# Seven-product down projection: units worked singly, finer operand splits, two of the six summed weight pieces kept in scratch slots

## The chip, the cores and the metric

The kernel runs on one core of one Trainium2 chip, as one launch. The metric is device time in microseconds (us), from the first to the last work of an execution. Five engines matter: TensorE (PE; its weight loads are listed apart as PEld), VectorE (DVE), ScalarE (ACT), GpSimd (POOL) and SyncE (SP), the last here only to issue plain transfers. Accumulating transfers are issued from GpSimd. All transfers run on the core's sixteen DMA engines.

## The reference

One decoder layer on 512 tokens of width 1024, in float32: RMS norm, one input projection, two mixers (a Mamba-2 SSD group and a forgetting-attention group), an output projection, a residual, and a gated MLP. The change is in the last part:

```python
def conv_gated_mlp(x, w_up, conv_w, conv_b, w_down):
    h = x @ w_up.astype(x.dtype)
    h = causal_depthwise_conv(h, conv_w, conv_b)
    gate, val = jnp.split(h, 2, axis=-1)
    return (jax.nn.silu(gate) * val) @ w_down.astype(x.dtype)

hf = rms_norm(x, norm_ffn_w[layer])
x = x + conv_gated_mlp(hf, w_up[layer], ffn_conv_w[layer], ffn_conv_b[layer], w_down[layer]).astype(x.dtype)
```

Here `w_up` is 1024 x 5632 and `w_down` is 2816 x 1024; the product with `w_down` is 512 x 2816 by 2816 x 1024.

## The kernel before

**Float32 from three passes.** Every large product splits both operands into a high part (a cast to float32r, on ScalarE) and a low part (the value less its high part, a subtraction on VectorE or GpSimd). `mm3` (L108) then does three matmuls: high by high (L110), high by low (L111), low by high (L112).

**The up projection** (`up_proj`, `gated`, `sums`, L734 to L787). 44 weight tiles of 512 KB go through `load_split` (L99): a load into one of five `wraw` slots, the cast and the subtraction. For each of the eleven values of j (L789) two tiles of the first half of the MLP's width and then two of the second half are projected, scaled by the token norm `R2`, convolved (L768 to L773) and gated (L775, and the product on GpSimd in L780 and L791). The result g is the left operand; its quarters over (first or second half of the tokens) x (first or second half of the 2816) are formed at once: `a11` and `a12` as high and low parts, `a22` and the four sums `S1` to `S4` as plain float32 (L792 to L794, L780 to L787). The squares for the token norm go into a scratch tile `junk` (L751), of the pool `pu`, which lives only as long as the up projection.

**The down projection** (L798 to L876) multiplies 2 x 2 blocks in seven products instead of eight. A weight quarter (B11, B12, B21, B22) is 1408 x 512: eleven k tiles, laid out as six units, five of two k tiles (512 KB) and one of a single k tile. `PRODUCTS` (L815) lists for each product its weight (a quarter, or None for the sum held in T), the next left operand, its two PSUM tiles, whether it starts or continues them, and where the result is added to `x2` (L874). Products 0, 1 and 6 read B11, B21 and B22 through `wraw` slots (`load_unit`, L713). Products 2 to 5 read T, six SBUF pieces that hold a running sum of quarters: `fresh` (L805) loads a quarter piece into T from SP, `gather` (L808) adds another one to it by an accumulating transfer from GpSimd. `next_sum` (L825) says which: B11 + B12 for product 2, then + B22 for product 3, + B21 for product 4, then B22 + B12 anew for product 5. (Signs lie in the left operands and in the additions.) A piece can be overwritten only when its split for the running product is done.

For each unit the loop of L844 calls `split_unit` (L720: cast on ScalarE, subtraction on VectorE, into one of three slots for `wh` and `wl`), then `next_sum`, then, at units 1 to 3, a third of the split of the next product's left operand (`split_into`, L755), and then the unit's matmuls, 12 for a unit of two k tiles. Units 4 and 5 are held and their 18 matmuls done together, ordered by output tile, at every product's end (L853 to L858). T is a pool of its own (L802), opened when `pu` has been closed.

**What sets the order.** The engines run their instructions in order. A planner lays out each engine's order before the run, from program order and from a timeline of its own; so a piece of work may stand earlier or later on its engine than its place in the program. SP and GpSimd have one queue each: what stands behind a waiting instruction waits too.

Of the kernel before, what the change touches and what calls it, by code (L numbers as in the profile page):

```python
# [8 lines left out]
F32 = mybir.dt.float32  # L9
F32R = mybir.dt.float32r  # L10
AF = mybir.ActivationFunctionType
ALU = mybir.AluOpType
# [3 lines left out]
P = 128  # L16
SEQ = 512
D = 1024
# [37 lines left out]
def tile_hybrid_layer(  # L56
# [19 lines left out]
    nc = tc.nc  # L76
# [11 lines left out]
    def raw(ap):  # L88
        return ap.bitcast(F32)
# [18 lines left out]
    def mm3(o, ah, al, bh, bl, start, stop, grouped=True):  # L108
        kw = {} if grouped else {"skip_group_check": True}
        pe.matmul(o, ah, bh, start=start, stop=False, **kw)  # L110
        pe.matmul(o, ah, bl, start=False, stop=False, **kw)  # L111
        pe.matmul(o, al, bh, start=False, stop=stop, **kw)  # L112

    def bank(name="g"):
        return pg.tile([P, 512], F32, tag="g", name=name)
# [572 lines left out]
    pb = ctx.enter_context(tc.tile_pool(name="pb", bufs=1, reuse_waits="tile"))  # L688
    NH = NFF // 2
# [3 lines left out]
    def operand(slot=None):  # L693
        if slot is None:
            hl_ = [pb.tile([P, NH, HT], F32R, tag=t, name=t, bufs=2) for t in ("oh", "ol")]
            return hl_[0], hl_[1]
        pair_ = [pxt.tile([P, NK, SEQ], F32R, tag=t, name="o" + t) for t in ("xh", "xl")]
        return tuple(
            t.rearrange("p a b -> p (a b)")[:, 0 : NH * HT].rearrange("p (a b) -> p a b", b=HT) for t in pair_
        )  # L700
# [6 lines left out]
    UNITS = [(k, min(k + 2, NH)) for k in range(0, NH, 2)]  # L707
    B11, B12, B21, B22 = 0, 1, 2, 3

    def part(q, u):  # L710
        return wdown[q, :, UNITS[u][0] * 512 : UNITS[u][1] * 512]

    def load_unit(q, u):  # L713
        rw = wp.tile([P, 1024], F32, tag="wraw", name="wraw", bufs=5)
        nc.sync.dma_start(rw[:, 0 : (UNITS[u][1] - UNITS[u][0]) * 512], part(q, u))
        return rw

    turn = [0]

    def split_unit(u, src):  # L720
        n = (UNITS[u][1] - UNITS[u][0]) * 512
        where = pb if turn[0] % 3 == 2 else wp
        turn[0] += 1
        h = where.tile([P, 1024], F32R, tag="wh", name="wh")
        l = where.tile([P, 1024], F32R, tag="wl", name="wl")
        act.copy(h[:, :n], src[:, :n])  # L726
        dve.tensor_tensor(out=l[:, :n], in0=src[:, :n], in1=raw(h[:, :n]), op=ALU.subtract)  # L727
        return h, l

    pu_ctx = ExitStack()  # L730
    pu = pu_ctx.enter_context(tc.tile_pool(name="pu", bufs=1, reuse_waits="tile"))
# [16 lines left out]

    early = up_proj((0, NFF), 2)
    for tb in range(NTB):  # L750
        junk = pu.tile([P, D], F32, tag="junk", name="junk", bufs=2)  # L751
        act.activation(junk, x2[:, tb, :], AF.Square, accum_out=ss[:, tb : tb + 1])
    token_scale(r2, R2, ss, pu)

    def split_into(o, src, lo, hi):  # L755
        act.copy(o[0][:, lo:hi, :], src[:, lo:hi, :])
        dve.tensor_sub(o[1][:, lo:hi, :], src[:, lo:hi, :], raw(o[0][:, lo:hi, :]))

    def gated(j):
        both = []  # L760
        for part in range(2):
            f = part * NFF + j
            o = early[part] if j == 0 else up_proj((f,), 1)[0]
            xp = pu.tile([P, SEQ], F32, tag="up", name="up", bufs=3)
            dve.tensor_mul(xp, o, R2)  # L765
            a = pu.tile([P, SEQ], F32, tag="ua", name="ua", bufs=5)
            cw = C_FCW + 3 * f
            act.activation(a, xp, AF.Identity, scale=pc[:, cw + 2 : cw + 3], bias=pc[:, C_FCB + f : C_FCB + f + 1])  # L768
            for s in range(1, 3):
                dve.scalar_tensor_tensor(  # L770
                    out=a[:, s:], in0=xp[:, : SEQ - s], scalar=pc[:, cw + 2 - s : cw + 3 - s], in1=a[:, s:],
                    op0=ALU.mult, op1=ALU.add,
                )  # L773
            both.append(a)
        act.activation(both[0], both[0], AF.Silu)  # L775
        return both

    def sums(j, g, k, val):
        g1, g2 = g[:, 0:HT], g[:, HT:]
        pool.tensor_tensor(out=k, in0=k, in1=val, op=ALU.mult)  # L780
        k1, k2 = k[:, 0:HT], k[:, HT:]
        act.copy(a12[0][:, j, :], k1)
        dve.tensor_sub(a12[1][:, j, :], k1, raw(a12[0][:, j, :]))
        act.copy(a22[:, j, :], k2)
        pool.tensor_tensor(out=S1[:, j, :], in0=g2, in1=k2, op=ALU.subtract)
        pool.tensor_tensor(out=S2[:, j, :], in0=S1[:, j, :], in1=g1, op=ALU.subtract)
        pool.tensor_tensor(out=S4[:, j, :], in0=k1, in1=S2[:, j, :], op=ALU.add)  # L787

    for j in range(NH):  # L789
        g, val = gated(j)  # L790
        pool.tensor_tensor(out=g, in0=g, in1=val, op=ALU.mult)  # L791
        act.copy(a11[0][:, j, :], g[:, 0:HT])  # L792
        dve.tensor_sub(a11[1][:, j, :], g[:, 0:HT], raw(a11[0][:, j, :]))
        pool.tensor_tensor(out=S3[:, j, :], in0=g[:, 0:HT], in1=g[:, HT:], op=ALU.subtract)  # L794
        k, val = gated(j + NH)
        if j < NH - 1:
            sums(j, g, k, val)
    ready = [split_unit(u, load_unit(B11, u)) for u in range(3)]  # L798
    sums(NH - 1, g, k, val)
    pu_ctx.close()  # L800

    pt_ = ctx.enter_context(tc.tile_pool(name="pt", bufs=1, reuse_waits="tile"))  # L802
    T = [pt_.tile([P, 512 * (b - a)], F32, tag="T%d" % a, name="T%d" % a) for a, b in UNITS]

    def fresh(q, u):  # L805
        nc.sync.dma_start(T[u], part(q, u))

    def gather(q, u):  # L808
        nc.gpsimd.dma_start(T[u], part(q, u), accum_op=ALU.add)

    Y, Z, X1, X2 = (
        [mbank("Y") for _ in range(2)], [mbank("Z") for _ in range(2)], [bank("X") for _ in range(2)], None
# [9 lines left out]
        (B22, S4, Z, False, ((0, 512, ADD, True),)),  # L822
    )

    def next_sum(n, u):  # L825
        if n == 0:
            fresh(B11, u)
            gather(B12, u)
        elif n in (2, 3):
            gather(B22 if n == 2 else B21, u)  # L830
        elif n == 4:
            fresh(B22, u)
            gather(B12, u)

    ops = [a11, a12]
    for n, (quarter, _, tiles, start, adds) in enumerate(PRODUCTS):
        nxt = PRODUCTS[n + 1][1] if n + 1 < len(PRODUCTS) else None
        if nxt is not None:
            ops.append(operand(1 if n % 3 == 1 else None))
        tiles = [bank("X") for _ in range(2)] if tiles is None else tiles  # L840
        lhs = ops[n]
        final = n == len(PRODUCTS) - 1
        held = []
        for u, (lo, hi) in enumerate(UNITS):  # L844
            if n == 0 and u < len(ready):
                h, l = ready[u]
            else:
                h, l = split_unit(u, T[u] if quarter is None else load_unit(quarter, u))
            next_sum(n, u)
            if nxt is not None and u in (1, 2, 3):  # L850
                split_into(ops[n + 1], nxt, 4 * (u - 1), min(4 * u, NH))
            held.append((lo, hi, h, l))
            if u == len(UNITS) - 2:  # L853
                continue
            todo = [(k, i, b) for b in held for k in range(b[0], b[1]) for i in range(2)]
            held = []
            if u == len(UNITS) - 1:
                todo.sort(key=lambda t: t[1])  # L858
            for k, i, (lo_, _, h_, l_) in todo:
                c = slice((k - lo_) * 512, (k - lo_ + 1) * 512)  # L860
                s = slice(i * P, (i + 1) * P)
                mm3(
                    tiles[i], lhs[0][:, k, s], lhs[1][:, k, s], h_[:, c], l_[:, c], start and k == 0, k == NH - 1,
                    grouped=False,
                )
                if k == NH - 1:
                    for row, col, op, done in adds:
                        tb = row + i
                        cuts = 2 if final and i == 1 else 1
                        w = 512 // cuts  # L870
                        for cut in range(cuts):
                            c = slice(cut * w, (cut + 1) * w)
                            oc = slice(col + cut * w, col + (cut + 1) * w)
                            dve.tensor_tensor(out=x2[:, tb, oc], in0=x2[:, tb, oc], in1=tiles[i][:, c], op=op)  # L874
                            if done:
                                nc.sync.dma_start(out[tb * P : (tb + 1) * P, oc], x2[:, tb, oc])  # L876
# [14 lines left out]
def _lay_out(i, np):  # L891
# [3 lines left out]
    def cols(v):  # L895
        return v.reshape(-1, 128).T

    def taps(v):
# [20 lines left out]
        "x": x,  # L919
        "xT": x.T.reshape(8, 128, 512),  # L920
        "wdtf": dtf.reshape(8, 128, 32).transpose(1, 0, 2).reshape(128, 256),
# [32 lines left out]
```

## Time and profile before

| | |
|---|---|
| median of 3 runs | 847.28 us (845.74 to 851.2) |
| the profiled execution | 845.59 us, span 843.8 us |
| granted TensorE clock | 0.998 |
| TensorE busy | 810.0 us (96%) |
| VectorE, ScalarE, GpSimd busy | 75%, 52%, 35% |
| up projection on TensorE | about 482 to 722.7 us |
| the seven products on TensorE | 722.7 to 839 us |
| accumulating transfers (T, from GpSimd) | 24: 20 of 512 KB, 4 of 256 KB |
| plain loads of T (from SP) | 12: 10 of 512 KB, 2 of 256 KB |

Times in the rows are microseconds from the span's start; the second number of a timeline row is the duration, and the bracket at its end gives the idle time before it and what ended that. In a row of a group stand busy time and mean nanoseconds of one. Matmuls are pipelined, so a busy TensorE isn't one at its peak: the steps from one matmul's start to the next tell more. In a table by windows the number in brackets is the count of instructions, and the DMA share is the mean busy share of the sixteen DMA engines, where overlapping packets can make it a little over 1.

### The profile page before, as it was taken

The numbers are of one execution on the slowest core, as the hardware profiler recorded it, in microseconds if no ns is written. First come the engines' busy times: TensorE is split into PE (matmuls) and PEld (weight loads), VectorE is DVE, ScalarE is ACT, GpSimd is POOL, SyncE is SP. The second block draws the span as 40 slices with busy tenths as digits, with TensorE's granted clock in tenths as the row PEclk, the third lists the DMA queues.
The fourth block names the chain that finished last, engine by engine and source line by source line (L and its number), as shares of the span: only waits on it lengthen the run. The fifth ranks groups of instructions, "written<-read, shape, count | busy, mean of one in ns | idle before, by whom it ended". The sixth has DMA issues, their size and how long they took to land.

```text
span 843.8 us, 12403 instructions
## 1 busy us (share of the span) xinstructions
PE 810.0 (96%) x4590; PEld 696.6 (83%) x4590; DVE 630.9 (75%) x999; ACT 434.6 (52%) x830; POOL 291.4 (35%) x281
## 2 busy tenths in 40 slices
PE   6999989899989999999999999999999999998987
PEld 4888879779989898798898888888888888875766
DVE  7696998775779788997988767666666667875644
ACT  5456546443567675684575364444444444654432
POOL 3125253375445445135133413333333331332210
PEclk9999999999999999999999999999999999999999
DMA  8424322431442332333331222322222333599972
GB/s 313 164 76 130 100 101 76 133 105 50 140 123 86 104 101 92 96 112 107 95 101 51 95 81 100 99 99 89 91 97 100 100 100 109 160 304 240 241 169 88
DMA packets 32285, 101.63 MB, mean 120 GB/s; under 512 B 4129, under 2 KB 4961, under 8 KB 32225
## 3 DMA queue, kind: packets, MB, share of 16 engines
q1 hardware_dynamic: 28768, 89.31, 32.3%
q0 software_dynamic: 3456, 11.54, 7.0%
q8 instruction: 36, 0.59, 0.3%
q14 instruction: 25, 0.20, 0.1%
HBM read 94.44 MB, written 2.20 MB: 115 GB/s over the span
## 4 chain that ended last, share of the span: by engine, by line
PE 67%; DVE 13%; issue 7%; DMA 6%; POOL 3%; ACT 3%; SPq 0%; DVEq 0%; POOLq 0%; ACTq 0%
PE up L112 9%; PE up L110 9%; PE up L111 9%; DMA T<-in_wdown_dram 4%; PE pq L111 4%; PE pq L112 4%; PE pq L110 4%; PE po L112 3%; PE po L111 3%; PE po L110 3%; DVE xs L351 2%; PE o L580 1%; PE pT L566 1%; POOL ms L122 1%; PE Y L111 1%
## 5 line engine op out<-in xcount | busy, mean ns | idle before, releaser
L104 ACT CAST wh<-wraw 128x1024 fp32r<-128x1024 f32 x103 | 108.4, 1053 | 135.5 <-PE up L111 72.1
L110 PE MATMUL pq<-wh,xh 128*128 128x256 f32 x512 | 146.3, 288 | 0.0
L112 PE MATMUL pq<-wh,xl 128*128 128x256 f32 x512 | 146.2, 286 | 0.0
L111 PE MATMUL pq<-wl,xh 128*128 128x256 f32 x512 | 145.3, 284 | 0.6 <-DVE wl L105 0.6
L112 PE MATMUL up<-hh,wl 128*128 128x512 f32 (+1 forms) x368 | 140.2, 381 | 0.2 <-DVE wl L105 0.2
L111 PE MATMUL up<-hl,wh 128*128 128x512 f32 (+1 forms) x368 | 139.9, 380 | 0.0
L110 PE MATMUL up<-hh,wh 128*128 128x512 f32 (+1 forms) x368 | 139.8, 380 | 0.0
L105 POOL TENSOR_TENSOR wl<-wraw,wh 128x1024 fp32r<-128x1024 f32 x31 | 75.3, 2427 | 107.7 <-ACT wh L104 98.6
L105 DVE TENSOR_TENSOR wl<-wraw,wh 128x1024 fp32r<-128x1024 f32 x72 | 90.3, 1254 | 20.0 <-ACT wh L104 19.9
L111 PEld LDWEIGHTS pq<-wl,xh 128*128 128x128 f32 x512 | 97.8, 191 | 2.1 <-DVE wl L105 1.1
L110 PEld LDWEIGHTS pq<-wh,xh 128*128 128x128 f32 x512 | 97.5, 191 | 1.9 <-issue 1.2
L112 PEld LDWEIGHTS pq<-wh,xl 128*128 128x128 f32 x512 | 97.8, 191 | 0.7 <-issue 0.5
L112 PEld LDWEIGHTS up<-hh,wl 128*128 128x128 f32 x368 | 69.2, 188 | 13.8 <-DVE wl L105 0.4
L111 PEld LDWEIGHTS up<-hl,wh 128*128 128x128 f32 x368 | 69.2, 188 | 13.1
L110 PEld LDWEIGHTS up<-hh,wh 128*128 128x128 f32 x368 | 69.1, 188 | 13.1 <-issue 0.2
L765 DVE TENSOR_TENSOR up<-up,R 128x512 f32<-128x512 f32 x44 | 30.3, 691 | 57.0 <-PE up L112 57.0
L770 DVE SCALAR_TENSOR_TENSOR ua<-up,pc,ua 128x511 f32<-128x511 f32 (+1 forms) x88 | 67.1, 765 | 3.2 <-ACT ua L768 1.7
L526 POOL TENSOR_SCALAR bias<-cum,tokS 128x256 f32<-128x256 f32 (+1 forms) x32 | 22.4, 711 | 88.9 <-DVE nm L541 88.9
L254 DVE TENSOR_TENSOR x<-po,x 128x512 f32<-128x512 f32 x64 | 43.2, 683 | 10.1 <-PE po L112 9.5
L545 ACT ACTIVATE prob<-prob,nm 128x128 f32<-128x128 f32 (+1 forms) x64 | 35.9, 562 | 27.2 <-DVE nm L541 26.9
L780 POOL TENSOR_TENSOR ua<-ua 128x512 f32<-128x512 f32 x11 | 15.0, 1364 | 93.0 <-DVE ua L770 93.0
L727 DVE TENSOR_TENSOR wl<-T,wh 128x1024 fp32r<-128x1024 f32 (+1 forms) x24 | 26.9, 1134 | 26.2 <-ACT wh L726 26.2
(249 smaller groups left out, 1876.9 us busy)
## 6 DMA issues: line engine op xcount, KB each, us to landing
wraw<-in_wup_dram SPq DMA_DIRECT2D x44, 512.0 KB, 3.3
wraw<-in_wqkv_dram SPq DMA_DIRECT2D x24, 512.0 KB, 3.3
T<-in_wdown_dram POOLq DMA_DIRECT2D x20, 512.0 KB, 11.9
wraw<-in_wout_dram SPq DMA_DIRECT2D x16, 512.0 KB, 3.4
wraw<-in_wdown_dram SPq DMA_DIRECT2D x15, 512.0 KB, 4.6
wraw<-in_wxbc_dram SPq DMA_DIRECT2D x11, 512.0 KB, 4.0
T<-in_wdown_dram SPq DMA_DIRECT2D x10, 512.0 KB, 8.0
wraw<-in_wz_dram SPq DMA_DIRECT2D x8, 512.0 KB, 3.4
```

Of the source, the lines that this page charges most:

```text
L104: act.copy(h, r)
L105: (sub or dve).tensor_tensor(out=l, in0=r, in1=raw(h), op=ALU.subtract)
L110: pe.matmul(o, ah, bh, start=start, stop=False, **kw)
L111: pe.matmul(o, ah, bl, start=False, stop=False, **kw)
L112: pe.matmul(o, al, bh, start=False, stop=stop, **kw)
L254: dve.tensor_add(dst, o, dst)
L351: dve.scalar_tensor_tensor(out=dst[:, s:], in0=xp[:, : SEQ - s], scalar=half_w[:, cw + 3 - s : cw + 4 - s], in1=dst[:, s:], op0=ALU.mult, ...
L526: (dve if qb == 2 else pool).tensor_scalar(out=b, in0=cum[:, :n], scalar1=-1.0, scalar2=edge, op0=ALU.mult, op1=ALU.add)
L545: act.activation(p, p, AF.Exp, scale=-1.0, bias=nm[:, qb : qb + 1], accum_out=sm[:, qb : qb + 1])
L727: dve.tensor_tensor(out=l[:, :n], in0=src[:, :n], in1=raw(h[:, :n]), op=ALU.subtract)
L765: dve.tensor_mul(xp, o, R2)
L770: dve.scalar_tensor_tensor(out=a[:, s:], in0=xp[:, : SEQ - s], scalar=pc[:, cw + 2 - s : cw + 3 - s], in1=a[:, s:], op0=ALU.mult, op1=ALU.add,
```

## The change

Three things in the down projection; the products, their order and their sums are the same.

1. Every unit's matmuls follow its own split. Units 4 and 5 are held together only in the last product.
2. The next left operand is split at every unit, by the unit's own k tiles: five pieces of 512 columns and one of 256, instead of pieces of 1024, 1024 and 768 columns at units 1 to 3.
3. `junk` moves from the pool `pu` to the lasting pool `pb`. After its last use its two slots hold T[0] and T[1], whose load and gather for product 2 (B11, then B12) are written into the program after the first three loads of B11 and before the last `sums`; T[2] to T[5] stay in the later pool.

```diff
+    T = []
+    def fresh(q, u):
+        nc.sync.dma_start(T[u], part(q, u))
+    def gather(q, u):
+        nc.gpsimd.dma_start(T[u], part(q, u), accum_op=ALU.add)
...
-        junk = pu.tile([P, D], F32, tag="junk", name="junk", bufs=2)
+        junk = pb.tile([P, D], F32, tag="junk", name="junk", bufs=2)
...
+        if j == NH - 2:
+            T = [pb.tile([P, 1024], F32, tag="junk", name="T", bufs=2) for _ in range(2)]
     ready = [split_unit(u, load_unit(B11, u)) for u in range(3)]
+    for u in range(2):
+        fresh(B11, u)
+        gather(B12, u)
     sums(NH - 1, g, k, val)
     pu_ctx.close()
...
-    T = [pt_.tile([P, 512 * (b - a)], F32, tag="T%d" % a, name="T%d" % a) for a, b in UNITS]
+    T += [pt_.tile([P, 512 * (b - a)], F32, tag="T%d" % a, name="T%d" % a) for a, b in UNITS[2:]]
...
+    ADDED = {0: B12, 2: B22, 3: B21, 4: B12}
     def next_sum(n, u):
+        if n == 0 and u < 2:
+            return
+        if n in (0, 4):
+            fresh(B11 if n == 0 else B22, u)
+        if n in ADDED:
+            gather(ADDED[n], u)
...
-            if nxt is not None and u in (1, 2, 3):
-                split_into(ops[n + 1], nxt, 4 * (u - 1), min(4 * u, NH))
+            if nxt is not None:
+                split_into(ops[n + 1], nxt, lo, hi)
             held.append((lo, hi, h, l))
-            if u == len(UNITS) - 2:
+            if final and u == len(UNITS) - 2:
                 continue
...
-            if u == len(UNITS) - 1:
+            if final and u == len(UNITS) - 1:
                 todo.sort(key=lambda t: t[1])
```

More of the change, by code (lines that the diff above doesn't have):

```diff
@@ L802, in tile_hybrid_layer @@
     pt_ = ctx.enter_context(tc.tile_pool(name="pt", bufs=1, reuse_waits="tile"))
-    T = [pt_.tile([P, 512 * (b - a)], F32, tag="T%d" % a, name="T%d" % a) for a, b in UNITS]
[L805 to L809, printed above, removed]
+    T += [pt_.tile([P, 512 * (b - a)], F32, tag="T%d" % a, name="T%d" % a) for a, b in UNITS[2:]]
     Y, Z, X1, X2 = (
@@ L823, in tile_hybrid_layer @@
     )
+    ADDED = {0: B12, 2: B22, 3: B21, 4: B12}
     def next_sum(n, u):
[L826 to L833, printed above, removed]
+        if n == 0 and u < 2:
[4 more added lines that the diff above has]
+            gather(ADDED[n], u)
     ops = [a11, a12]
```

## The prediction

> **What bounds the kernel now.** I read the page first, then the chain of waits, then the last 120 us in 8 us windows, then each engine's and each DMA queue's order in time there.
>
> ```profile
> span 843.8 us, 12403 instructions
> core 0: 843.8 us, clock 0.998
> ```
>
> The profiled execution took 845.59 us, 1.8 us more than its span; the median of the three timed runs is 847.28. The granted clock is full, so nothing here is a matter of the clock. The chain shows the matmul rhythm and the limits of the down stage:
>
> ```profile
> 540.44 0.23 PE up L110
> 554.72 0.23 PE up L110
> 722.68 0.45 PE Y L110 x2
> 838.72 0.24 PE Z L112
> 755.89 17.31 DMA T<-in_wdown_dram
> 800.65 11.36 DMA T<-in_wdown_dram
> ```
>
> The first two rows are 63 matmuls apart (L110 is every third): 14.28 / 63 = 0.2267 us each. The seven products hold 7 x 11 x 2 x 3 = 462 matmuls, 104.7 us; they take from 722.68 to 838.96, 116.3 us. So TensorE loses 11.5 us in this stage, and that is all an edit of the operand traffic can win. Where it loses them:
>
> ```profile
> core 0: us, PE busy (x) PEld busy (x) DVE busy (x) ACT busy (x) POOL busy (x), PEclk, DMA share, GB/s
> 724.00:732.00 8.00, 8.00 (x37) 6.57 (x36) 7.10 (x8) 4.92 (x7) 2.25 (x2) 1.00 0.49 135
> 740.00:748.00 8.00, 7.62 (x34) 5.95 (x33) 6.32 (x6) 3.29 (x4) 4.93 (x6) 1.00 1.05 328
> 756.00:764.00 8.00, 7.62 (x33) 5.77 (x32) 5.04 (x5) 2.54 (x3) 2.47 (x3) 1.00 1.06 276
> 764.00:772.00 8.00, 6.79 (x26) 4.27 (x24) 2.76 (x3) 2.72 (x3) 1.70 (x2) 1.00 1.08 252
> 772.00:780.00 8.00, 6.13 (x25) 4.34 (x25) 7.20 (x9) 5.68 (x6) 1.70 (x2) 1.00 1.06 211
> 788.00:796.00 8.00, 7.62 (x33) 5.93 (x33) 7.07 (x8) 5.58 (x6) 0.00 (x0) 1.00 1.05 257
> 804.00:812.00 8.00, 5.64 (x22) 3.52 (x21) 3.65 (x4) 2.09 (x2) 1.73 (x2) 1.00 1.07 244
> ```
>
> An unhindered window starts 37 matmuls. Against that, 764 to 780 lacks 23 (5.2 us), 804 to 812 lacks 15 (3.4 us), and 740, 756 and 788 lack 3, 4 and 4 (2.5 us together). The DMA share is at 1.05 to 1.08 in all of them, against 0.49 before: the sixteen DMA engines are full. So the two large losses are waits for T, and the whole stretch is a DMA backlog that TensorE drains.
>
> **The change, part by part.** *The DMA ledger.* The price of one 512 KB unit, from stretches where one queue has the engines nearly alone (775 to 787 for the accumulating queue, which has them quite alone; 735 to 745 for loads):
>
> ```profile
> q0 software_dynamic: 762, 2.52, 107.1%
> q1 hardware_dynamic: 994, 3.27, 91.3%
> q0 software_dynamic: 33, 0.14, 7.2%
> ```
>
> A gather: 2.52 MB in 12 us is 0.210 MB/us, so 0.524 MB take 2.50 us. A plain load: 3.27 MB in 10 x 91.3 / 98.5 = 9.27 us, so 1.49 us. [...]
>
> The backlog starts when the first T pieces are loaded and ends when the last gathered piece is cast:
>
> ```profile
> 732.79 4.36 SPq L806 DMA_DIRECT2D T<-in_wdown_dram  x6
> 818.36 0.62 ACT L726 CAST wh<-T 128x512 fp32r<-128x512 f32 x1 [0.19 <-DMA T<-in_wdown_dram]
> ```
>
> In those 85.6 us the queues carry two plain quarters into T (11 units), half of B21's last unit pair and five units of B22 fetched ahead (5.5), one unit of output, and four gathered quarters (22): 17.5 x 1.49 + 22 x 2.50 = 81.1 us. The other 4.5 us are loads already in flight at 732.8 and completion. It is a saturated queue from end to end.
>
> *What is moved.* T[0] and T[1] get the scratch slots of `junk`, and their load and gather (B11 + B12, units 0 and 1) stand in the program before the last `sums`. The slots are long free, and SP has room:
>
> ```profile
> L752 ACT ACTIVATE junk<-x x4: 1045/1050/1065, 485.4 to 488.6; 128x1024 f32<-128x1024 f32 x4
> 703.07 6.77 SPq L715 DMA_DIRECT2D wraw<-in_wdown_dram  x2
> L806 SPq DMA_DIRECT2D T<-in_wdown_dram x12: 327/379/946, 732.8 to 800.1; - x12
> DMA to landing us min/median/max: 4.4/8.5/11.6
> 716.92 1.30 POOL L791 TENSOR_TENSOR ua<-ua 128x512 f32<-128x512 f32 x1 [8.52 <-DVE ua L770]
> ```
>
> The third of the three loads that precede them goes out at 703.07; two more issues of 0.38 us follow, land between 708 and 715.5 (4.4 to 11.6 us later), and their gathers run under the up projection, where the DMA share is about half (the 0.49 above). That takes 2 x (1.49 + 2.50) = 8.0 us out of the ledger. The new wait is GpSimd's: a gather waits for its load, and the gate products (L791, L780) and the last sums are queued behind it. Landed by 715.5, they come before L791's start at 716.92. If SP lets one more load ahead (the second of the two in that row, at 709.5) and the maximum of 11.6 us applies, L791 starts some 4 us late, at 721; its result is the eleventh k of product 0, wanted at 722.68 + 60 x 0.2267 = 736.3. I cost it at nothing under that cover of 15 us; without it the 4 us would stand in product 0.
>
> *Units worked singly.* Now units 4 and 5 (18 matmuls) are held together at every product's end and both their operand slots come free at the end; then unit 4's slot comes free 6 matmuls, 1.36 us, earlier. *Smaller splits.* The split of the next left operand goes from pieces of 1024, 1024 and 768 columns at units 1 to 3 to five of 512 and one of 256 at units 0 to 5. The wall it makes today:
>
> ```profile
> 739.68 3.22 DVE L757 TENSOR_TENSOR ol<-sum,oh 128x1024 fp32r<-128x1024 f32 x3
> 742.82 3.49 DVE L727 TENSOR_TENSOR wl<-wraw,wh 128x1024 fp32r<-128x1024 f32 x3
> 744.10 0.50 PE L111 MATMUL X<-wl,oh 128*128 128x512 f32 x1 [0.39 <-DVE wl L727]
> L757 DVE TENSOR_TENSOR ol<-sum,oh 128x1024 fp32r<-128x1024 f32 x4 | 4.7, 1218 | 0.0
> 733.88 0.96 DVE L757 TENSOR_TENSOR oxl<-sum,oxh 128x768 fp32r<-128x768 f32 x1 [0.62 <-ACT oxh L756]
> L727 DVE TENSOR_TENSOR wl<-T,wh 128x512 fp32r<-128x512 f32 x4 | 2.8, 688 | 1.3 <-ACT wh L726 1.3
> 697.52 0.42 DVE L793 TENSOR_TENSOR ol<-ua,oh 128x256 fp32r<-128x256 f32 x1
> ```
>
> Three pieces in a row stand ahead of the next wl, and TensorE waits: that is the loss in 740, 756 and 788. VectorE's cost rises from 2 x 1.22 + 0.96 = 3.40 to 5 x 0.69 + 0.42 = 3.87 us a product, 2.3 us over five products; it is 3 to 7 of 8 us busy in the windows above, so this lies in its idle time, and where that cover is gone it is at most 0.47 us a product. The additions into x2 start now 3 instead of 9 matmuls before a product's end; today they stand in VectorE's order behind the whole product anyway, so nothing is charged. Breaking the wall is worth 0 to 2.5 us by itself, less than nothing only in the slow rival.
>
> *The sum.* TensorE's side offers up to 11.5 us, the backlog's side 8.0: the stage ends with the later, so the gain is 8.0. The losses at the walls then hide in the wait for the DMA, as long as it stays full. It should: a gather issued at 755.89 lands 17.3 us later today, nearly all of it queueing; 8 us less leaves 9 us of queue. What is late next is again product 5: unhindered it would begin at 722.68 + 5 x 14.96 = 797.5 (66 matmuls a product), and its last T piece arrives at 818.4 - 8.0 = 810.4, against a need near 797.5 + 60 x 0.2267 - 1.3 = 809.8; so a small wait stays there. Profiled time 845.59 - 8.0 = 837.6; on the median, 847.28 - 8.0 = **839.3**.
>
> **The rivals.**
>
> *TensorE becomes the bound.* Loads of B22 into T go out today at
>
> ```profile
> 787.60 0.34 SPq L806 DMA_DIRECT2D T<-in_wdown_dram  x1
> 800.13 0.33 SPq L806 DMA_DIRECT2D T<-in_wdown_dram  x1
> 796.77 0.86 POOL L809 DMA_DIRECT2D T<-in_wdown_dram  x1 [11.35 <-DMA T<-in_wdown_dram]
> 805.31 1.04 ACT L726 CAST wh<-T 128x1024 fp32r<-128x1024 f32 x1 [5.94 <-DMA T<-in_wdown_dram]
> ```
>
> with a spread of 12.5 us, because the pieces of product 4 came late. Without walls and late sums they go out sooner against the product, the gathers of product 5 meet fewer of them, and all waits vanish: 847.28 - 11.5 = 835.8.
>
> *The load-and-gather chain of product 5 is latency, not queue.* From the load at 787.60 to the cast at 805.31 are 17.7 us, and the load cannot go before product 4 has split T[0]. If those 17.7 us stay, so do product 5's 3.4 us, and with the walls half kept (1.3 us) the gain is 11.5 - 4.7 = 6.8; with the walls whole and a wait of 1 us at each of the units 1 to 3 it is 3: 840.5 to 844.3. [...]
>
> *The early sums are not early.* The planner may place the two loads as late as it does today, behind the loads of B21:
>
> ```profile
> 732.40 0.33 SPq L715 DMA_DIRECT2D wraw<-in_wdown_dram  x1
> ```
>
> Then only the walls can give: 0 to 2.5 us, 845 to 847.
>
> *Slower.* The six small pieces stand one behind each unit's cast on in-order queues. A slot has two units, 5.44 us, from free to needed; a cast and a subtraction with a piece ahead of each need 1.05 + 0.62 + 1.23 + 0.69 = 3.6. If the planner puts two more pieces ahead and the slot's release adds 0.5, TensorE waits on most of the 30 units of products 1 to 5. At 0.27 us each that eats the 8.0; from 0.55 us it is slower by 8.5, and at 0.6 the time is 847.28 - 8.0 + 18 = 857. Against it: the wall of 3.22 us costs TensorE about 0.7 us today, not more.
>
> **How the numbers follow.** The forecast 0.50, with gains from 6 to 10; TensorE as the bound 0.18; latency 0.18; not early 0.08; slower 0.06. One per cent, about what a measurement of this kernel can tell from no change, is 8.5 us, just above the forecast: four tenths of the forecast's own chance lie beyond it. So faster by over 1% is 0.18 + 0.20 and a little for the runs' spread, 0.40; within 1% 0.54; slower 0.06. The range runs from the TensorE bound, 835.8, to the bad end of the latency case, 844.5.
>
> **What would show it.** Product 2's last T piece is cast now at
>
> ```profile
> 766.65 0.62 ACT L726 CAST wh<-T 128x512 fp32r<-128x512 f32 x1 [1.37 <-DMA T<-in_wdown_dram]
> ```
>
> Right: two loads and two gathers of T before 722; that cast near the time it is needed, 752.6 + 12.3 = 764.9, without waiting for a DMA, and no TensorE wait in products 2 and 3; the last T cast near 810; DMA share still above 1 from 740 to 805; no row of three splits in VectorE's order. It is wrong if T still ends near 818 with the first two sums early, if the DMA share falls below 1 in products 3 and 4 (then the stage is TensorE's), or if waits for wl stand at every unit.

## The result and the profile after

The changed kernel takes 841.11 us (median; 838.15 to 844.77) against 847.85 us (845.74 to 851.98) for the kernel before in the same series: a ratio of 0.9912, 95% interval 0.9892 to 0.9931. By the ratio that is 7.4 us, with an interval of 5.9 to 9.2 (6.7 between the medians), where 8.0 was forecast. The profiled execution took 841.84 us. Two executions, one of e8 and one of e9 below, took over 4 ms, and the medians given for these two leave them out.

The page of the kernel after, its first line, and then its table by windows of 8 us (columns as before: busy time and count of PE, PEld, DVE, ACT and POOL, granted clock, DMA share, GB/s):

```profile
span 840.1 us, 12435 instructions
```

```profile
740.00:748.00 8.00, 8.00 (x37) 6.54 (x36) 7.80 (x12) 5.10 (x8) 3.50 (x4) 1.00 1.02 299
756.00:764.00 8.00, 8.00 (x37) 6.56 (x36) 7.27 (x10) 4.21 (x6) 3.24 (x5) 1.00 1.07 277
764.00:772.00 8.00, 8.00 (x37) 6.56 (x36) 4.71 (x6) 5.36 (x8) 2.41 (x3) 1.00 1.07 232
772.00:780.00 8.00, 8.00 (x36) 6.57 (x35) 6.42 (x9) 3.44 (x6) 3.49 (x4) 1.00 1.07 208
788.00:796.00 8.00, 8.00 (x36) 6.57 (x35) 5.59 (x7) 2.44 (x3) 2.59 (x3) 1.00 0.95 264
796.00:804.00 8.00, 5.09 (x18) 3.35 (x17) 1.82 (x2) 1.04 (x1) 0.86 (x1) 0.83 1.05 257
804.00:812.00 8.00, 8.00 (x28) 6.34 (x27) 3.59 (x4) 3.14 (x3) 1.76 (x2) 0.74 1.04 193
```

From 740 to 796 TensorE misses nothing: 36 or 37 matmuls in each window, where before 23 were missing between 764 and 780 alone. Then one hole opens in the window from 796, and, new in this stage, the granted clock falls (0.83 and 0.74 in the last two windows). Where the time went is plainest in the starts of the products, counted from product 0's first matmul (rows of TensorE; an unhindered product takes 15.1 us):

| us from product 0's start | product 1 | 2 | 3 | 4 | 5 | 6 | last matmul |
|---|---|---|---|---|---|---|---|
| before | 15.08 | 30.85 | 48.66 | 66.66 | 83.89 | 101.24 | 116.49 |
| after | 15.08 | 30.20 | 45.32 | 60.44 | 78.59 | 96.89 | 111.80 |

From the starts of products 1 and 4 on: products 1 to 3 took 51.6 us and take 45.4, so 6.2 us came back. Products 4 and 5 together took 34.6 us and take 36.5: they lose 1.9 us more than they did. With 0.3 us from product 6 the stage (here and below: from the start of product 0's first matmul to the start of the last matmul) is 4.7 us shorter. (Product 0 itself started 0.9 us later in this profile, 723.45 against 722.52, before anything that the change touches on TensorE; over all profiles of this study it starts between 720.8 and 729.3. So stages are compared from product 0's start, and 4.7 - 0.9 is the 3.8 us between the two profiled times.)

How product 5 begins, in the timeline of the kernel after (start, duration; in the bracket the idle time before and what ended it):

```profile
782.31 12.59 SPq L721 DMA_DIRECT2D T<-in_wdown_dram  x6
791.24 0.86 POOL L724 DMA_DIRECT2D T<-in_wdown_dram  x1 [11.40 <-DMA T<-in_wdown_dram]
798.77 0.40 PE L112 MATMUL X<-wh,ol 128*128 128x512 f32 x1
800.95 1.04 ACT L734 CAST wh<-T 128x1024 fp32r<-128x1024 f32 x1 [7.12 <-DMA T<-in_wdown_dram]
802.04 1.22 PE L110 MATMUL Y<-wh,oxh 128*128 128x512 f32 x2 [2.87 <-ACT wh L734]
805.18 0.63 PE L110 MATMUL Y<-wh,oxh 128*128 128x512 f32 x1
805.60 0.63 PE L111 MATMUL Y<-wl,oxh 128*128 128x512 f32 x1
814.08 0.62 ACT L734 CAST wh<-T 128x512 fp32r<-128x512 f32 x1 [0.20 <-DMA T<-in_wdown_dram]
```

The reload of T[0] goes out at 782.31, as soon as product 4 has split that piece; its gather can start 8.9 us later, and the cast 9.7 us after that: 18.6 us for the chain, against 17.7 before. Product 4's last matmul starts at 798.77 and TensorE has nothing until 802.04. Then matmuls follow each other by 0.42 us instead of 0.227.

### The profile page after: what moved, and what is told of

It is laid out like the page before. It is cut to its first block, busy times and chain, and to the rows that moved or that the text cites. A ratio compares the mean times of both kernels' runs of the same rounds, so it can differ in the third digit from the quotient of the medians.

```text
span 840.1 us, 12435 instructions
## 1 busy us (share of the span) xinstructions
PE 810.9 (97%) x4590; PEld 701.1 (83%) x4590; DVE 631.6 (75%) x1014; ACT 436.1 (52%) x845; POOL 291.8 (35%) x281
## 4 chain that ended last, share of the span: by engine, by line
PE 72%; DVE 11%; issue 7%; DMA 4%; POOL 3%; ACT 2%; SPq 0%; DVEq 0%; POOLq 0%; ACTq 0%
PE up L112 9%; PE up L110 9%; PE up L111 9%; PE pq L111 4%; PE pq L112 4%; PE pq L110 4%; PE po L110 3%; PE po L112 3%; PE po L111 3%; DVE xs L351 2%; DMA T<-in_wdown_dram 2%; PE Y L110 2%; PE Y L111 2%; PE Y L112 2%; PE yd L415 2%
```

## The experiments

Theory A: the two early sums empty the DMA queue earlier, and this is the whole gain; the small pieces and the units worked singly only keep TensorE from waiting where nothing else does. Theory B, the rival: units and pieces give a good part of the gain. For what is left at product 5: theory A says that the chain of a load, a gather and a cast holds it up, a rival says that the queue is still full.

**The parts alone.** e1 keeps the single units and small pieces and puts the sums back, and `junk` and all of T into their old pools with them (no run moves `junk` alone):

```diff
-        junk = pb.tile([P, D], F32, tag="junk", name="junk", bufs=2)
+        junk = pu.tile([P, D], F32, tag="junk", name="junk", bufs=2)
...
-        if j == NH - 2:
-            T = [pb.tile([P, 1024], F32, tag="junk", name="T", bufs=2) for _ in range(2)]
...
-    for u in range(2):
-        fresh(B11, u)
-        gather(B12, u)
...
-        if n == 0 and u < 2:
-            return
```

> The changed kernel with T[0] and T[1] loaded and gathered late again, as in the kernel before (units singly and small splits stay). Theory (the stage is a DMA backlog, and the gain is the 8 us of transfers taken out of it): the last cast of T stays about 96 us behind the first matmul of product 0 (818.4 - 722.7 before), the walls' 2.5 us turn into a longer wait for T, and the time is 846 to 848. Rival (VectorE's and ScalarE's walls were the loss): 2.5 us or more are gained without the early sums, 845 or less.

Measured: 846.74 us, ratio 0.9991 (0.9972 to 1.0011); stage 115.4 us against 116.5. The last cast of T comes 95.1 us behind product 0's first matmul (95.8 before). The windows of e1:

```profile
740.00:748.00 8.00, 8.00 (x37) 6.57 (x36) 6.09 (x8) 3.12 (x5) 4.76 (x6) 1.00 1.04 343
764.00:772.00 8.00, 7.22 (x29) 5.13 (x29) 2.14 (x4) 2.71 (x3) 2.56 (x3) 1.00 1.09 247
772.00:780.00 8.00, 6.53 (x27) 4.77 (x28) 7.26 (x10) 5.95 (x9) 1.71 (x2) 1.00 1.06 211
```

The loss at the wall in 740 to 748 is gone. The waits for T in 764 to 780 stand (56 matmuls of 74; 51 before), and so does the time: most of what the walls gave up, the backlog took.

e2 is the opposite, early sums with the old units and pieces; e11 is the same kernel in another series:

```diff
-            if nxt is not None:
-                split_into(ops[n + 1], nxt, lo, hi)
+            if nxt is not None and u in (1, 2, 3):
+                split_into(ops[n + 1], nxt, 4 * (u - 1), min(4 * u, NH))
...
-            if final and u == len(UNITS) - 2:
+            if u == len(UNITS) - 2:
...
-            if final and u == len(UNITS) - 1:
+            if u == len(UNITS) - 1:
```

> The kernel before with the early load and gather of T[0] and T[1] alone: units 4 and 5 held together at every product's end, splits in three large pieces. Theory (DMA backlog): nearly the whole gain, 841 to 842.5, with TensorE's three short waits behind the split pieces (0.7 us each) back and the wait before product 5 shorter by as much. Rival (walls): 843.5 to 845.5, the wait before product 5 as long as in the changed kernel.

> The early sums alone, once more. The stage took 110.2 us here and 111.8 and 110.3 in two executions of the changed kernel, but the medians were 842.2 against 841.1 and 840.4. If the other two edits give nothing while T is late: 840 to 841.5 and 110 to 111 us. If they give something that one execution does not show: 842 to 843.

Measured: 842.21 us, 0.994 (0.9916 to 0.9964), and 841.87 us, 0.9932 (0.9906 to 0.9959); stages 110.2 and 111.4. The changed kernel itself, once more beside e5 to e7:

> The changed kernel once more, beside the others. 840 to 842; the wait before product 5 again 2.5 to 3.5 us with half clock behind it, if the gap is a matter of the order of work and not of one execution.

Measured: 839.84 us, 0.9909 (0.9878 to 0.994), stage 110.3 (after: 111.8). So the early sums bring 5 to 6 us by themselves. What units and pieces add on top is 0.8 to 2.4 us by the medians, 1.7 to 2.6 us by the ratios and nothing in the stage; the intervals overlap, and this stays open. The windows of e2 show the walls, with DMA behind them:

```profile
740.00:748.00 8.00, 7.62 (x33) 5.94 (x33) 7.52 (x8) 6.43 (x7) 3.33 (x4) 1.00 1.01 345
764.00:772.00 8.00, 8.00 (x36) 6.57 (x36) 3.14 (x4) 2.34 (x3) 3.64 (x5) 1.00 1.06 243
772.00:780.00 8.00, 7.62 (x33) 5.93 (x33) 7.98 (x9) 5.96 (x7) 1.66 (x2) 1.00 1.08 211
804.00:812.00 8.00, 7.14 (x29) 4.87 (x28) 3.29 (x4) 2.59 (x3) 2.63 (x3) 1.00 1.06 253
```

The walls cost 3 or 4 matmuls a product, as before; the waits of products 2 and 3 are gone; product 5 still waits. As product 5 waits for its data in any case, time saved at the walls ends in that wait.

**What holds product 5.** e5 leaves out the reload of B22 for product 5, so that its gather can go as soon as the piece is split; the product's weight is then another one.

```diff
-        if n in (0, 4):
-            fresh(B11 if n == 0 else B22, u)
+        if n == 0:
+            fresh(B11, u)
```

> The changed kernel without the load of B22 into T for product 5: B12 is gathered onto the old sum, so that product has the wrong weight and only its time counts. It takes 5.5 units, 8.2 us, of plain loads and one landing out of the chain behind each piece. Theory (product 5 waits because a load and a gather must follow one another through a full queue): no wait before product 5, 75.5 us from the first matmul of product 0 to product 5's instead of 78.6, no half clock, about 105.6 us to the last matmul, 835 to 836. Rival (the gathers alone are too slow for a product's 15 us): a wait of 1 us or more stays, 838 or more.

e3 exchanges products 5 and 6 in the table, so that product 6, which reads B22 through `wraw`, runs while the new sum is formed; e12 is the same kernel in another series.

```diff
 PRODUCTS:
-        (None, S3, Y, False, ((2, 0, ADD, True), (2, 512, SUB, True))),
         (B22, S4, Z, False, ((0, 512, ADD, True),)),
+        (None, S3, Y, False, ((2, 0, ADD, True), (2, 512, SUB, True))),
```

> The changed kernel with products 5 and 6 exchanged: the one on B22 from the raw slots first, the last one on T = B22 + B12. Theory (the 6 us that TensorE loses in product 5 are a wait for T and what follows from it): T has 15 us more, TensorE never waits in the seven products, and it ends near 828.5 instead of 835.2; the last product now has two additions and two stores per tile instead of one, about 1 us, so 835 to 836. Rival (T is late by more than a product, or the end grows by as much): no faster than 839.

> The changed kernel with products 5 and 6 exchanged, once more: 836 to 837.5, no wait, 105.6 us, 4 us or so under the changed kernel.

Measured: e5 835.86 us, 0.9865 (0.9826 to 0.9904), stage 105.55. e3 836.89 us, 0.9889 (0.9861 to 0.9916), stage 105.58; e12 838.95 us, 0.9911 (0.9886 to 0.9935), stage 105.60. Windows of e5, and then of e3:

```profile
788.00:796.00 8.00, 8.00 (x36) 6.58 (x36) 6.67 (x9) 3.61 (x6) 3.38 (x4) 1.00 1.07 209
796.00:804.00 8.00, 8.00 (x36) 6.55 (x36) 4.78 (x5) 4.02 (x4) 0.13 (x1) 1.00 0.98 191
```

```profile
788.00:796.00 8.00, 8.00 (x37) 6.56 (x36) 5.36 (x7) 2.73 (x3) 2.59 (x3) 1.00 0.98 262
796.00:804.00 8.00, 8.00 (x37) 6.54 (x36) 5.12 (x6) 3.53 (x4) 1.62 (x2) 1.00 1.06 265
804.00:812.00 8.00, 8.00 (x37) 6.55 (x36) 3.13 (x3) 2.37 (x4) 1.00 (x2) 1.00 0.91 187
```

TensorE waits nowhere in e3, at the same DMA load and with the same reload: with 15 us more, the chain is hidden. In e5, without the load, the gathers alone are in time, though they fill the queue (DMA share 1.07 and 0.98 in its two windows). So product 5's wait is for the reload and the gather behind it. Whether by their landings one after the other or by the queue is not shown by these two: e5 takes 8.2 us of loads (5.5 x 1.49) out of the queue together with one landing from each chain, and e3 gives time for either. The DMA share of the kernel after speaks for the queue: in windows of 2 us from 782 to 812 it is 0.97 to 1.09, but for 792 to 796 with 0.86. So each step of the chain passes through a queue that is nearly full. By the rows of TensorE the exchange takes 4.7 to 6.2 us from the stage. It pays some of that back behind it, since the product that is now last has six additions into `x2` to do after the last matmul and not three. VectorE's last rows, in e3 and in the kernel after:

```profile
827.95 2.61 DVE L881 TENSOR_TENSOR x<-x,Y 128x512 f32<-128x512 f32 x6 [5.08 <-PE Y L112]
```

```profile
835.22 1.35 DVE L881 TENSOR_TENSOR x<-x,Z 128x512 f32<-128x512 f32 x3 [5.08 <-PE Z L112]
```

From the last matmul's start to the span's end it is 6.3 us in e3 (827.97 to 834.3) and 4.85 in the kernel after (835.25 to 840.1). That leaves 3 to 5 us. By the medians e3 is 3.0 to 4.2 us under the changed kernel (839.84 and 841.11) and e12 0.9 to 2.2; the intervals of the ratios overlap with those of the changed kernel. The exchanged kernel has the shorter stage in both profiles; its gain in time over the changed kernel is settled no better than 0 to 4 us.

**The clock.** e4 lets TensorE work through the hole: twelve more matmuls with a zero operand, added to the last sum of product 4, which they leave as it is.

```diff
...
+                if (n, i, k) == (4, 1, NH - 1):
+                    fill = lhs[0].rearrange("p a b -> p (a b)")[:, 0:512]
+                    for d in range(12):
+                        pe.matmul(tiles[i], zero, fill, start=False, stop=d == 11, skip_group_check=True)
```

> The changed kernel with twelve matmuls by a zero tile at the end of product 4's second sum, 2.7 us of work that adds nothing, in the gap in which TensorE waits for T. It asks what the half clock after the gap (0.50 granted from 802 to 808) costs. If the clock is lost to the gap and product 5 is paced by T's pieces landing 3.9, 3.2 and 2.4 us apart, full clock is worth 0.5 to 1 us: 840 to 840.7. If the half clock is the cost, its 14 matmuls at 0.43 instead of 0.23 us, 2.8 us are gained: about 838.3. If the clock falls all the same (matmuls by zero do not hold it), no change from 841.1.

Measured: 839.74 us, 0.9911 (0.9886 to 0.9935), stage 109.5 (after: 111.8 and 110.3). Windows of e4:

```profile
796.00:804.00 8.00, 7.90 (x35) 6.08 (x33) 2.99 (x3) 2.10 (x2) 1.75 (x2) 1.00 1.06 252
804.00:812.00 8.00, 7.52 (x32) 5.88 (x33) 4.12 (x5) 3.77 (x4) 0.88 (x1) 1.00 0.79 153
```

The clock stays at 1.00, and product 5 takes 16.2 us instead of 18.3 (17.6 in e8). But T's pieces still arrive one by one, so full clock mostly turns into waiting; the stage is 0.8 to 2.3 us shorter, and the ratio shows no difference from the changed kernel.

**Walls and units where nothing hides them.** With products 5 and 6 exchanged, TensorE is the bound, and what units and pieces are worth can be seen. e6 has neither of the two edits, e7 only the units, e9 only the small pieces. e7's edit against e3 is the first pair of lines below, e9's the other two pairs, and e6's all of them:

```diff
-            if nxt is not None:
-                split_into(ops[n + 1], nxt, lo, hi)
+            if nxt is not None and u in (1, 2, 3):
+                split_into(ops[n + 1], nxt, 4 * (u - 1), min(4 * u, NH))
...
-            if final and u == len(UNITS) - 2:
+            if u == len(UNITS) - 2:
...
-            if final and u == len(UNITS) - 1:
+            if u == len(UNITS) - 1:
```

> Products 5 and 6 exchanged and the early sums, but units 4 and 5 held together at every product's end and the splits in three large pieces, as before the change. With no wait for T left, the walls lie open. Theory (the walls cost 0.77 us in each of products 1 to 4 and a little in 5, and were hidden in the wait for T): 3 to 4 us over the exchanged kernel with all three edits, 840 to 841, down stage 108.6 to 109.6 us. Rival (units and pieces cost as much as they give): 837 to 838.

> Products 5 and 6 exchanged, early sums, units worked singly, but splits in three large pieces at units 1 to 3. It tells the two parts of the edit apart. If the freed slot of unit 4 is what removes the wall: as with all three edits, 836.5 to 837.5. If the small pieces do it: walls of 0.5 us or more in products 1 to 4 remain, 839 or more. My guess is between: the slot, with waits of 0.2 us or less.

> Products 5 and 6 exchanged, early sums, small splits, but units 4 and 5 held together at every product's end. If the small pieces alone remove the walls, as e7_swap_large says: 105.6 us from product 0's first matmul to the last, no wait, 836 to 838. If units worked singly are needed with them: waits of 0.3 us or more in products 1 to 4, 107 or more.

| exchanged, early sums | units | pieces | stage, us | median, us | ratio |
|---|---|---|---|---|---|
| e3, e12 | singly | small | 105.58, 105.60 | 836.89, 838.95 | 0.9889, 0.9911 |
| e9 | held | small | 105.70 | 837.38 | 0.991 (0.9873 to 0.9946) |
| e7 | singly | large | 108.14 | 840.79 | 0.992 (0.9888 to 0.9952) |
| e6 | held | large | 108.11 | 840.2 | 0.9906 (0.9877 to 0.9935) |

The stage goes by the pieces alone, with one or two profiles for each row: 2.5 us more with large ones, as large as the prediction's upper bound for the walls, and nothing for the units (0.1 us). My guess that the units would share in it fell. In e6 products 1 to 4 take 15.7 us each instead of 15.1. One of these waits in TensorE's timeline:

```profile
741.36 0.62 PE L110 MATMUL X<-wh,oh 128*128 128x512 f32 x2
742.36 0.50 PE L111 MATMUL X<-wl,oh 128*128 128x512 f32 x1 [0.38 <-DVE wl L735]
```

The second row comes 1.00 us after the pair of the first, which without a wait takes 2 x 0.227: some 0.55 us lost to one subtraction that stood behind the wall. In the medians the 2.5 us are not resolved.

**Exchange without early sums.** e10 is e3 with e1's edit.

> Products 5 and 6 exchanged, units singly, small splits, but T[0] and T[1] loaded and gathered late. Theory (the backlog stands in products 2 and 3 too): the waits before product 5 of e1_late_sums stay, 82.6 - 75.5 = 7.1 us less the 0.5 at its start, then none: 112 us, 843 to 844. Rival (only product 5's sum is too late): 105.6 to 107 us, 837 to 838.

Measured: 843.75 us, 0.9964 (0.9947 to 0.9981), stage 112.5: TensorE waits again in products 2 and 3, as the windows of e10 show, and nowhere later.

```profile
764.00:772.00 8.00, 6.95 (x28) 5.10 (x28) 2.13 (x3) 2.19 (x3) 2.56 (x3) 1.00 1.07 256
772.00:780.00 8.00, 6.89 (x22) 5.24 (x23) 6.08 (x9) 5.42 (x9) 1.71 (x2) 0.79 1.07 216
788.00:796.00 8.00, 8.00 (x37) 6.56 (x36) 6.65 (x9) 6.03 (x9) 0.00 (x0) 1.00 1.06 243
```

So the two cures are for two waits: early sums end those of products 2 and 3 (112.5 to 105.6), the exchange that of product 5.

## Why the prediction was right, and where it was not

**The size and its source.** Forecast 8.0 us from the early sums, units and pieces hidden; measured 7.4 (5.9 to 9.2) for all three edits, 0.8 (-0.9 to 2.4) for units and pieces alone (e1), 5 to 6 for the early sums alone (e2, e11). That the gain comes from the early sums stands. That 7.4 lies so near to 8.0 is in part luck: in the profiles the stage is 4.7 us (after) and 6.2 us (e8) shorter, and where the rest of the 7.4 lies is not shown.

**The early sums are early, and earlier than I said.** I put their loads behind the third load of B11, at about 703 to 709, and spent a paragraph on whether GpSimd's gate product would wait behind the gathers. The timeline of the kernel after:

```profile
489.63 1.36 SPq L721 DMA_DIRECT2D T<-in_wdown_dram  x2
493.83 2.98 SPq L101 DMA_DIRECT2D wraw<-in_wup_dram  x2
493.68 1.07 POOL L724 DMA_DIRECT2D T<-in_wdown_dram  x1 [1.74 <-DMA T<-in_wdown_dram]
495.82 0.86 POOL L724 DMA_DIRECT2D T<-in_wdown_dram  x1 [1.07 <-DMA T<-in_wdown_dram]
```

The planner sends them as soon as the slots are free, right behind the last use of `junk`, more than 200 us ahead of the third load of B11 (703.07 in the kernel before), behind which they stand in the program. GpSimd waits there for 2.8 us in all, far from any gate product. The conclusion (free) was right for another reason. I had read the slots as free at 488.6 and not asked whether the loads would move there.

**The ledger's 8.0 us were too many.** The rows of the two queues (packets, MB, share) and of the B units' loads between 733 and 818, before and then after:

```profile
q0 software_dynamic: 3456, 11.54, 69.2%
q1 hardware_dynamic: 3138, 10.10, 33.3%
wraw<-in_wdown_dram SPq DMA_DIRECT2D x5, 512.0 KB, 16.4
```

```profile
q0 software_dynamic: 3168, 10.49, 63.8%
q1 hardware_dynamic: 2940, 9.36, 31.9%
wraw<-in_wdown_dram SPq DMA_DIRECT2D x6, 512.0 KB, 9.5
```

1.05 MB of gathers fewer, as counted, but only 0.74 MB of plain loads: SP has two T loads fewer to send ahead of the B quarters, but one more unit of those (six instead of five, in the last rows) falls into the stretch. At the prediction's own prices that is 5.0 + 2.1 = 7.1 us. By the shares in the same rows it is less: 5.4% of 85 us, 4.6 us, for the gathers and 1.4%, 1.2 us, for the loads, 5.8 us together. The term that the forecast rests on was too large by 1 to 2 us.

**Product 5: the first piece, not the last.** I wrote that the backlog "should" stay, since 9 us of queue would be left, and that product 5 would keep "a small wait", with its last T cast at 810.4. From product 0's start that is 87.9 us; it came at 90.6 (after), 90.0 (e8), 89.0 (e4), against 95.8 us before: 5.2 to 6.9 us earlier, not 8.0, and near the 5.8 of the shares. The DMA share did fall to 0.95 in the window from 788 to 796, which I had named as a sign that the queue no longer decides. But in the windows of 2 us the fall is short: four us at 0.86, some 0.6 us of engine time. So the queue stayed nearly full, as I had written, and still the wait was not small, because I had compared only the last piece with its need. The hole of 3.3 us is at the first piece: T[0] was cast 77.5 us from product 0's start, when product 4's matmuls had ended near 75.6. The reload of T[0] can't go before product 4 has split that piece, and its chain was no shorter than before: the latency rival had 17.7 us from the load to the cast, and it is 18.6. In that the rival was right, and the loss around product 5 stayed, as it said; "not queue" is not shown (e5 and e3 above). The rival's price (a gain of 6.8 with the walls half kept) and the forecast's (8.0) lie too near each other for the time to tell them apart; the stage in the two profiles, 4.7 and 6.2 us shorter, is nearer to the rival's.

**The walls.** That their losses "then hide in the wait for the DMA": right as measured (e2 against after: 110.2 and 111.4 against 111.8 and 110.3), where the wait left is the one at product 5. Their size, 2.5 us, was right to the tenth where they can be seen (e6 against e3). The "row of three splits" did not vanish quite as I said. VectorE's timeline after:

```profile
740.62 2.49 DVE L765 TENSOR_TENSOR ol<-sum,oh 128x512 fp32r<-128x512 f32 x4
743.02 1.22 DVE L735 TENSOR_TENSOR wl<-wraw,wh 128x1024 fp32r<-128x1024 f32 x1
744.16 1.02 DVE L765 TENSOR_TENSOR ol<-sum,oh 128x512 fp32r<-128x512 f32 x2
```

The planner puts four of the six pieces in a row, 2.49 us instead of 3.22, and TensorE doesn't wait. The slower rival (a piece ahead of every unit's subtraction, 0.27 us and more for each) has no row to show for it in products 0 to 4.

**TensorE as the bound** was half right: it is, through product 4, and in e3 to the end. There the whole 10.9 us that the stage lost against 105.6 are back.

**The clock was not in the sum.** I had written that nothing here is a matter of the clock. That was true of before, whose waits at product 5 came in three pieces: 1.70, 1.26 and 1.26 us from one row of TensorE's timeline to the next. Now they come in one piece, and what it costs is below.

## What to carry to other kernels

A transfer taken out of a saturated queue need not bring its whole price: here 8.0 us by the ledger moved the last piece by 5.2 to 6.9. What is late then can be a load that cannot be issued earlier because its buffer is still being read (T[0] for product 5, 18.6 us from load to cast); follow its whole chain, load and gather and cast, for the first piece as well as for the last. Here the chain was hidden by giving it another product's time, a matter of the order of the work, at the same traffic (e3: a stage of 105.6 us instead of 111.8 and 110.3). Small edits on an engine off the path show nothing while a later wait absorbs them (here stages of 110.2 and 111.4 us without them, 111.8 and 110.3 with them), and their full size once that wait is gone (2.5 us, e6 against e3); judge them after it, in the stage and not in the whole kernel's time.

## What the hardware showed that I had not expected

One hole of 3 us cost more than its 3 us: with it filled (e4), product 5 took 16.2 us instead of 18.3. The windows of 2 us of the kernel after, behind the last matmul of product 4 (798.77):

```profile
800.00:802.00 2.00, 0.00 (x0) 0.00 (x0) 0.00 (x0) 1.04 (x1) 0.60 (x1) 0.82 1.06 262
802.00:804.00 2.00, 1.92 (x4) 1.10 (x5) 1.82 (x2) 0.00 (x0) 0.26 (x1) 0.50 1.08 251
806.00:808.00 2.00, 2.00 (x6) 1.58 (x5) 1.72 (x2) 0.01 (x1) 0.04 (x1) 0.50 1.03 198
808.00:810.00 2.00, 2.00 (x9) 1.57 (x9) 0.94 (x1) 1.03 (x1) 0.88 (x1) 0.97 1.05 203
```

In a hole of 3.27 us from one row of TensorE's timeline to the next, the granted clock falls at 801.3 (0.82 in the first window), 2.1 us after the end of the last matmul (798.77 + 0.40). It is 0.50 for 6.8 us, and the matmuls come every 0.42 us (805.18 to 805.60 above). e8 had 2.58 and 1.26 us one behind the other, and then 0.50 for 3.4 us. Two pairs of shorter holes differ: before had 1.70 and 1.26 us one behind the other at product 5, at a clock of 1.00; e10 had 1.37 and 1.26 one behind the other at 771.20, and its clock fell (0.79 in the window above). So 2.63 us of holes in a short stretch went with a fall (e10) and 2.96 us with none (before). What tells the two apart no run here shows.

In the clock records of the kernel after, the clock falls at 163.0, 238.1 and 801.3 us. These falls are 75.1 and 563.2 us apart, 22 and 165 times the 3.413 us for which the first two stretches at 0.50 last; the third lasts 6.83 us, twice as long.
